# Both expert layers: 32 of 256 tokens by indexed fetch of their chosen rows, 224 dense, the weighted sum made features-by-tokens

## The chip, the cores and the metric

One NeuronCore of one Trainium2 chip runs the whole program. TensorE (PE, with its weight loads shown apart as PEld), VectorE (DVE), ScalarE (ACT), GpSimd (POOL) and SyncE (SP) have an instruction queue each; transfers between HBM and the on-chip memory run on 16 DMA engines. The metric is device microseconds of one execution, as the median of several runs. A second number, the span, is the time from the first to the last instruction of one profiled execution.

## The reference, cut to what matters

The program is two transformer blocks on 256 tokens of 1024 features, all in float32. Each block has an attention mixer and an expert layer; the change touches the two expert layers alone. An expert layer chooses 16 of 16,384 experts for each token and head (8 heads), 128 in all for a token, and sums their value rows:

```python
v1, i1 = lax.top_k(s1, PEER_TOPK)
v2, i2 = lax.top_k(s2, PEER_TOPK)
...
sc, pos = lax.top_k(cand, PEER_TOPK)
eidx = jnp.take_along_axis(cidx, pos, axis=-1)
g = jax.nn.softmax(sc, axis=-1)
u = jnp.take(expert_u, eidx, axis=0)
a = jnp.einsum('thkd,td->thk', u, hc).astype(jnp.float32)
act = (jax.nn.gelu(a, approximate=False) * g).astype(hc.dtype)
vv = jnp.take(expert_v, eidx, axis=0)
return jnp.einsum('thk,thkd->td', act, vv)
```

An expert's number is 128 times its place in the first list plus its place in the second, so the experts form a 128 by 128 grid. `expert_u` and `expert_v` are 64 MB each in each layer.

## The kernel before, in words

The tokens are two tiles of 128. Every expert is computed for every token, and the gate of an expert that a token did not choose is zero. Weights come in units of 128 by 1024 float32 (512 KB), in one long list for the whole program. SP loads them into four `raw` buffers (L290). Each unit is split into two float32r parts: ACT copies `hi` (L302), DVE subtracts to get `lo` (L311), two units ahead of their use. A product is three passes, hi by hi, hi by lo, lo by hi (L330, L331, L332 in `mm3`).

An expert layer (`peer`) goes through these stages:

- Queries: the products of the normed tokens with the query weights, then scores against the keys.
- The u stage: 128 blocks of 128 experts. For each block `project_t` takes a unit of `expert_u`; for each of 8 chunks of features it makes three products, with the unit's chunk as the stationary operand and all 256 tokens as the moving one: 24 products of 256 columns a block. Two blocks share a PSUM bank, and `activated` applies Gelu (L279 by way of `curve`, L1029).
- Meanwhile `top_k` chooses the experts in small steps on DVE, a few of them after each block (lists L1142 to L1146 and what follows). When it is through ("chosen"), `group` makes the gates of four tokens at a time: one-hot rows of the two lists (ACT L997, L998; DVE L1002, L1003), eight float16 products of 128 columns on PE (L1009, L1010), and the product with what is already there of the activations, in `ga` (ACT L1016, DVE L1018). `ga` holds, for each of the 128 blocks, 128 experts by 256 tokens, 128 KB a partition. There are 64 groups, spread over the blocks up to block 122.
- The v stage: 128 blocks again. For each, a unit of `expert_v` is the moving operand in two halves of 512 columns, and the weights in `ga`, split in two parts by `weigh` (ACT L323, DVE L324), are stationary, one tile of 128 tokens at a time (L1073): 12 products of 512 columns a block. The sums come out as tokens by features in four PSUM banks, and are added to x (L509).

Nothing but program order sets who runs when: generators ("tasks") are stepped once after each block by `tick`, and each step records instructions on several engines. An engine works through its own instructions strictly in the recorded order, so an instruction that waits holds up all that stands behind it on its engine. In the last layer the first tile's sums end early, and its last norm and way out run beside the second tile's products.

Of the kernel before, what the change touches and what calls it, by code (L numbers as in the profile page):

```python
# [19 lines left out]
TILES = 2  # L20
# [4 lines left out]
# the second mixer's features, in the order in which they are made  # L25
# [3 lines left out]
# (quarter of the columns, half of k) of an output projection  # L29
# [3 lines left out]
def _columns():  # L33
    """Column ranges of the two packed arrays of constants and small inputs."""
    off, table = 0, {}
    for name, n in (("ident", 128), ("norm_mix", 8), ("norm_ffn", 8), ("norm_ple", 8), ("norm1", 8),
                    ("norm2", 8), ("norm_o", 8), ("b_gate", 2), ("na_q", 1), ("na_k", 1), ("dil_q", 64),
                    ("dil_k", 64), ("cos", 16), ("sin", 16), ("vmask", 8), ("kmask", 32), ("ends", 2)):
# [14 lines left out]
def mixed(lists):  # L53
    """Independent chains of steps, taken in turns."""
    return [step for steps in zip(*lists) for step in steps]

# [16 lines left out]
# The tokens are kept in the order (t % 2, t % 32 // 2, t // 32): a tile holds every second token, so that it holds  # L73
# whole classes of the two wider dilations, and every second one of its rows lies in the same half of the grid's columns.
# [8 lines left out]
def _arrays(a):  # L83
    """Device inputs: the reference's arrays laid out, and constants that depend on shapes alone."""
# [16 lines left out]
    o["meta"] = np.ascontiguousarray(np.asarray(a["meta_tokens_2"], f))  # L101
    o["normf"] = np.ascontiguousarray(np.asarray(a["norm_f_g_2"], f).reshape(1, 1024))
# [9 lines left out]
    # the branches of the first half of the columns first  # L112
# [10 lines left out]
    for i, (un, vn) in enumerate((("peer_expert_u", "peer_expert_v"), ("expert_u_2", "expert_v_2"))):  # L123
        u = np.asarray(a[un], f)[0].reshape(128, 128, 8, 128)
        o[f"u{i + 1}"] = np.ascontiguousarray(u.transpose(0, 3, 2, 1)).reshape(128, 128, 1024)
        o[f"v{i + 1}"] = np.ascontiguousarray(np.asarray(a[vn], f)[0]).reshape(128, 128, 1024)
# [11 lines left out]
    # neighbourhood attention: a half of the grid's columns at a time, and the near quarter of the other half  # L138
# [11 lines left out]
    # dilated attention: all keys, and twice those of the same tile  # L150
# [33 lines left out]
    put(cst, "ends", np.stack([p % 64 >= 48, p % 64 < 16], axis=1))  # L184
    o["cst"] = cst
# [29 lines left out]
class Kernel:  # L215
# [668 lines left out]
    def peer(self, gain, keys, sides_apart, aim, prefetch):  # L884
# [197 lines left out]
        for blk in range(128 - n_last):  # L1082
# [8 lines left out]
            if self.tasks:  # L1091
                self.tick()
# [743 lines left out]
```

## Time and profile before

| what | value |
|---|---|
| timed runs | 2031.79, 2033.11, 2036.97 us; median 2033.11 us |
| profiled execution | span 2031.8 us, 35290 instructions |
| PE busy | 2015.8 us, 13710 matmuls |
| DVE busy | 1448.3 us |
| ACT busy | 1153.0 us |
| POOL busy | 7.6 us |
| DMA | 344.00 MB, mean 169 GB/s |
| u stage, first and second layer | from 277 to 676 us, from 1264 to 1665 us |
| v stage, first and second layer | from 676 to 1035 us, from 1665 to 2024 us |

The profiled execution's span lies at the low end of the three timed runs. "Busy" of PE counts a matmul from its start to its modelled end, and matmuls overlap, so the rate has to be read from how many start in a stretch and not from the share. The starts of the stages are the first and last matmuls of L330 and L1073.

### The profile page before, as it was taken

To read this page: it belongs to the slowest core of one execution; us is meant where nothing else is said; L and a number is where in the kernel's file an instruction comes from. 1 tells how busy PE (TensorE), PEld (TensorE's weight loads), DVE (VectorE), ACT (ScalarE), POOL (GpSimd) and SP (SyncE) were. 2 spreads that over 40 slices of the span, in tenths; PEclk is the share of its full clock that TensorE was granted. 3 is DMA by queue.
4 is the path that set the end of the run, shared out by engine and by line. 5 is a ranking of instruction groups with operands and counts; after the bars stand their busy time and mean duration, and the time that the engine had idled before them with its cause. 6 is when DMAs were issued, how large, how long until landed. Compare 5 with 4: busy or idle time off the path is not lost.

```text
span 2031.8 us, 35290 instructions
## 1 busy us (share of the span) xinstructions
PE 2015.8 (99%) x13710; PEld 1822.6 (90%) x13710; DVE 1448.3 (71%) x3074; ACT 1153.0 (57%) x1867; POOL 7.6 (0%) x14
## 2 busy tenths in 40 slices
PE   8999999999999999999999999999999999999998
PEld 7899999999999888888879989999999998888886
DVE  6866899778889555555576568997889985555555
ACT  5555556577776544444465645465777764444444
POOL 1000000000000000000000000000000000000000
PEclk9999999999999999999999999999999999999999
DMA  7443455544444555565654314555444445555563
GB/s 247 150 152 110 165 177 181 191 156 161 162 166 157 189 185 190 183 196 183 198 191 142 104 52 160 184 177 191 152 160 160 159 170 192 183 191 186 186 202 130
DMA packets 95703, 344.00 MB, mean 169 GB/s; under 512 B 10640, under 2 KB 11936, under 8 KB 95536
## 3 DMA queue, kind: packets, MB, share of 16 engines
q1 hardware_dynamic: 93168, 337.16, 49.5%
q10 hardware_dynamic: 2368, 4.60, 0.7%
q8 instruction: 107, 1.75, 0.3%
q14 instruction: 60, 0.49, 0.1%
HBM read 340.66 MB, written 1.05 MB: 168 GB/s over the span
## 4 chain that ended last, share of the span: by engine, by line
PE 96%; DVE 2%; ACT 1%; issue 0%; DMA 0%; SPq 0%; DVEq 0%; ACTq 0%
PE bank L1073 35%; PE bank L330 18%; PE bank L331 17%; PE bank L332 17%; PE bank L1009 2%; PE bank L1010 1%; PE bank L1661 1%; DVE lo L311 1%; PE bank L489 1%; PE bank L431 0%; PE bank L736 0%; ACT hi L302 0%; PE bank L949 0%; PE bank L682 0%; DMA x<-in_x_dram 0%
## 5 line engine op out<-in xcount | busy, mean ns | idle before, releaser
L302 ACT ACTIVATE hi<-raw 128x1024 fp32r<-128x1024 f32 x639 | 676.4, 1060 | 772.7 <-PE bank L1073 369.9
L311 DVE TENSOR_TENSOR lo<-raw,hi 128x1024 fp32r<-128x1024 f32 x639 | 773.9, 1221 | 231.2 <-ACT hi L302 230.2
L330 PE MATMUL bank<-ht,hi 128*128 128x256 f32 x2336 | 668.9, 286 | 0.0
L331 PE MATMUL bank<-ht,hi 128*128 128x256 f32 x2336 | 655.7, 281 | 0.0
L332 PE MATMUL bank<-ht,lo 128*128 128x256 f32 x2336 | 655.2, 280 | 0.0
L1073 PE MATMUL bank<-hi,ht 128*128 128x512 f32 x2048 | 561.9, 395 | 0.0
L1073 PEld LDWEIGHTS bank<-hi,ht 128*128 128x128 f32 x2048 | 384.3, 188 | 94.8
L330 PEld LDWEIGHTS bank<-ht,hi 128*128 128x128 f32 x2336 | 440.6, 189 | 1.7 <-ACT hi L302 0.3
L331 PEld LDWEIGHTS bank<-ht,hi 128*128 128x128 f32 x2336 | 440.6, 189 | 0.0
L332 PEld LDWEIGHTS bank<-ht,lo 128*128 128x128 f32 x2336 | 439.9, 188 | 0.0
L1073 PE MATMUL bank<-lo,ht 128*128 128x512 f32 x1024 | 323.4, 395 | 0.0
L1073 PEld LDWEIGHTS bank<-lo,ht 128*128 128x128 f32 x1024 | 192.2, 188 | 45.1
L324 DVE TENSOR_TENSOR ht<-ga,ht 128x1024 fp32r<-128x1024 f32 (+2 forms) x78 | 84.1, 1088 | 149.8 <-ACT ht L323 149.7
L1003 DVE TENSOR_SCALAR o<-iota,i1t,pack 128x128 f32<-128x128 f16 x512 | 163.9, 341 | 0.0
L1018 DVE SCALAR_TENSOR_TENSOR ga<-bank,ga 128x216 f32<-128x216 f32 (+30 forms) x128 | 64.9, 507 | 44.4 <-ACT ga L1016 43.6
L997 ACT ACTIVATE away<-iota,i2t 128x128 f16<-128x128 f16 x256 | 87.4, 391 | 0.0
L330 PE MATMUL bank<-hi,ht 128*128 128x512 f32 (+1 forms) x224 | 82.7, 369 | 0.0
L331 PE MATMUL bank<-lo,ht 128*128 128x512 f32 (+1 forms) x224 | 80.7, 360 | 0.8 <-DVE lo L311 0.8
L332 PE MATMUL bank<-hi,ht 128*128 128x512 f32 (+1 forms) x224 | 80.5, 359 | 0.6 <-DVE ht L424 0.6
L1009 PE MATMUL bank<-o,o 128*128 128x128 f16 x512 | 74.3, 223 | 0.0
L323 ACT ACTIVATE ht<-ga 128x1024 fp32r<-128x1024 f32 (+2 forms) x78 | 72.4, 936 | 0.7 <-PE bank L332 0.3
L1010 PE MATMUL bank<-o,o 128*128 128x128 f16 x512 | 72.6, 218 | 0.0
(338 smaller groups left out, 1875.3 us busy)
## 6 DMA issues: line engine op xcount, KB each, us to landing
raw<-in_u_dram SPq DMA_DIRECT2D x256, 512.0 KB, 3.5
raw<-in_v_dram SPq DMA_DIRECT2D x256, 512.0 KB, 4.2
raw<-in_w_qkv_dram SPq DMA_DIRECT2D x30, 512.0 KB, 4.2
raw<-in_w_q_dram SPq DMA_DIRECT2D x24, 512.0 KB, 3.5
raw<-in_w_t_dram SPq DMA_DIRECT2D x21, 512.0 KB, 3.5
raw<-in_w_gates_dram SPq DMA_DIRECT2D x16, 512.0 KB, 3.5
raw<-in_w_branch_dram SPq DMA_DIRECT2D x14, 512.0 KB, 3.5
raw<-in_w_pg_dram SPq DMA_DIRECT2D x8, 512.0 KB, 4.2
```

The costliest lines, as they stand in the source:

```text
L302: self.nc.scalar.activation(parts[0], raw, AF.Copy)
L311: self.nc.vector.tensor_tensor(lo, raw, hi.bitcast(F32), op=OP.subtract)
L323: self.nc.scalar.activation(hi, src, AF.Copy)
L324: self.nc.vector.tensor_tensor(lo, src, hi.bitcast(F32), op=OP.subtract)
L330: mm(out, l[0], r[0], start=start, stop=False, **kw)
L331: mm(out, l[0], r[1], start=False, stop=False, **kw)
L332: mm(out, l[1], r[0], start=False, stop=stop, **kw)
L997: nc.scalar.activation(away[:, j], self.iota, AF.Abs, scale=-1.0, bias=i2t[:, 4 * g + j:4 * g + j + 1])
L1003: nc.vector.tensor_scalar(o1[:, j], self.iota, i1t[:, t:t + 1], pf[:, t:t + 1], op0=OP.is_equal, op1=OP.mult)
L1009: nc.tensor.matmul(b[:, j], o2[:, j], halves[:, :, 1], start=True, stop=False)
L1010: nc.tensor.matmul(b[:, j], o2[:, j], halves[:, :, 0], start=False, stop=True)
L1073: nc.tensor.matmul(acc[tt][n], weights[i][:, ai, j, s], v[vi][:, n], start=blk == 0 and ai == 0 and vi == 0, stop=blk == 127 and ai == 1)
```

## The change

Of the 256 tokens the first 224 (`DENSE`) stay in the dense scheme, the last 32 (`GATHERED`) leave it.

For the 224: the moving operand of the u products is 224 columns, not 256; `ga` is 224 tokens wide; there are 56 groups of gates, not 64. In the v stage the operands change places: a chunk of 128 features of the `expert_v` unit is stationary, and the weights of 224 tokens move. One product of 448 columns takes hi of v with both parts of the weights, and one of 224 columns takes lo of v with hi of the weights; the sums stand as features by tokens in eight PSUM banks, all there are, and are turned back by transposes at the end.

For the 32: `spread_picks` repeats each token's chosen expert numbers and gates four times over the partitions, so that partition 32 g + t holds the picks 32 g to 32 g + 31 of token t. `gathers` then fetches, for each of 32 picks, a [128, 1024] tile of rows of `expert_u` by an indirect DMA from GpSimd (512 KB, a new row-major copy `rows1`, `rows2` in HBM), and DVE reduces its product with the normed tokens to one number a partition. After Gelu and gates, 32 more indirect DMAs fetch rows of `expert_v`, which DVE sums up, weighted. Three buffers hold fetched rows; a reduction comes after every third `tick` in the u stage and after every second one in the v stage. The four shares of each token are added by one product with the constant `fold`. The early end of the first tile in the last layer is gone. (The rest of the diff drops comments and docstrings, so line numbers move.)

```diff
+GATHERED = 32
+DENSE = 256 - GATHERED
+SHARE = 128 // GATHERED
...
-    def project_t(self, ht, out):
+    def project_t(self, ht, out, s=slice(None)):
         w = self.unit(8)
         for k in range(8):
-            self.mm3(out, (w[0][:, k], w[1][:, k]), both(ht, k), k == 0, k == 7)
+            self.mm3(out, (w[0][:, k], w[1][:, k]), both(ht, k, s), k == 0, k == 7)
         self.tick()
...
-        ga = pool.tile([128, 128, 256], F32, name="ga")
+        ga = pool.tile([128, 128, DENSE], F32, name="ga")
...
+        picks = self.ready_picks(pool, n)
...
+        n_groups = DENSE // 4
+        self.start(self.gathers(pool, picks, n))
         for blk in range(128):
...
-            self.project_t(ht, b[:, blk % 2])
+            self.project_t(ht, b[:, blk % 2], dense)
...
-        acc = [[self.bank() for _ in range(2)] for _ in range(TILES)]
+        acc = [self.bank()[:, :2 * DENSE].rearrange("p (s t) -> p s t", s=2) for _ in range(8)]
...
-            for ai, vi in ((0, 0), (0, 1), (1, 0)):
-                for n in halves:
-                    nc.tensor.matmul(acc[tt][n], weights[i][:, ai, j, s], v[vi][:, n],
-                                     start=blk == 0 and ai == 0 and vi == 0, stop=blk == 127 and ai == 1)
+            mm = nc.tensor.matmul
+            mm(acc[c], v[0][:, c], weights[i][:, :, j], start=blk == 0, stop=False, skip_group_check=True)
+            mm(acc[c][:, 1], v[1][:, c], weights[i][:, 0, j], start=False, stop=blk == 127, skip_group_check=True)
...
-        self.drain()
+        self.done.add("second")
+        self.run_until_idle("gathers")
...
+        self.until("summed")
...
+        for c in range(8):
+            for blk, v in last:
+                add_rows(blk, v, c)
+            nc.scalar.activation(corr[:, c], acc[c][:, 1], AF.Copy)
+            nc.vector.tensor_tensor(out[:, c], acc[c][:, 0], corr[:, c], op=OP.add)
+            if c % 4 == 3:
...
+                nc.tensor.matmul(banks[1][128 - GATHERED:, :], self.c("fold"), picks["sum"][:, s], start=True, stop=True)
+                for k in range(4):
+                    for tt in range(TILES):
...
+                        nc.tensor.transpose(banks[tt][:rows, 128 * k:128 * (k + 1)], out[:, 4 * half + k, ts], ident)
+                for tt in range(TILES):
+                    self.add_to_x(tt, 512 * half, banks[tt])
...
         if aim is None:
-            for _ in second:
+            for _ in mixed_steps(self.finish(0), self.finish(1)):
                 pass
...
+    def spread_picks(self, picks, numbers, gates):
...
+        for j, t in enumerate((numbers, gates)):
+            mm(b[:, j], repeat, t, start=True, stop=True)
+        mm(b[:, 2, :TILES], repeat, self.y, start=True, stop=True)
+        yield
+        for g in range(SHARE):
+            rows = slice(GATHERED * g, GATHERED * (g + 1))
+            nc.vector.tensor_copy(picks["index"][rows], b[rows, 0, rows])
+            nc.scalar.activation(picks["gate"][rows], b[rows, 1, rows], AF.Copy)
...
+    EVERY = (3, 2)
+    def gathers(self, pool, picks, n):
...
+        for half in range(2):
+            s = slice(512 * half, 512 * (half + 1))
+            b = self.bank()
+            nc.tensor.matmul(b, self.c("repeat"), self.x[:, 1, s], start=True, stop=True)
+            yield
+            h = picks["normed"][:, s]
+            nc.vector.scalar_tensor_tensor(h, b, picks["y"][:, 1:2], h, op0=OP.mult, op1=OP.mult)
+        tables = (self.d[f"rows{n}"], self.d[f"v{n}"].rearrange("b p d -> (b p) d"))
+        jobs = [(t, j) for t in range(2) for j in range(GATHERED)]
...
+                rows[i] = pool.tile([128, 1024], F32, tag="gathered", name="gathered", bufs=3)
+                nc.gpsimd.indirect_dma_start(out=rows[i], out_offset=None, in_=tables[t],
+                                             in_offset=bass.IndirectOffsetOnAxis(ap=picks["index"][:, j:j + 1], axis=0))
...
+        for i, (t, j) in enumerate(jobs):
+            for _ in range(self.EVERY["second" in self.done]):
+                yield
+            r = rows.pop(i)
+            if t == 0:
+                nc.vector.tensor_tensor_reduce(r, r, picks["normed"], 1.0, 0.0, OP.mult, OP.add, w[:, j:j + 1])
+            else:
+                if j == 0:
...
+                    nc.vector.tensor_scalar(total, r, w[:, :1], None, op0=OP.mult)
+                else:
+                    nc.vector.scalar_tensor_tensor(total, r, w[:, j:j + 1], total, op0=OP.mult, op1=OP.add)
+            fetch(i + 3)
```

How the recorded order moves is seen at three places. First DVE late in the first layer's u stage, before: `lo` is a unit's second part, `o` a one-hot row of a gate group, `ga` the gates or activations.

```order
L311 TENSOR_TENSOR lo<-raw,hi 128x1024
L1018 SCALAR_TENSOR_TENSOR ga<-bank,ga 128x110x4
L1029 TENSOR_TENSOR ga<-ga,bank 128x2x220
L1003 TENSOR_SCALAR o_8183<-iota,i1t,pack 128x128 x2
L1002 TENSOR_SCALAR o_8182<-iota,i2t 128x128
L1003 TENSOR_SCALAR o_8183<-iota,i1t,pack 128x128
L1002 TENSOR_SCALAR o_8182<-iota,i2t 128x128
L1003 TENSOR_SCALAR o_8183<-iota,i1t,pack 128x128
L311 TENSOR_TENSOR lo<-raw,hi 128x1024
```

And now, at about the same block:

```order
L334 TENSOR_TENSOR lo<-raw,hi 128x1024
L1216 ISA gathered,pick_dot<-gathered,repeated 128x1024
L1216 ISA pick_dot 128x1
L1043 SCALAR_TENSOR_TENSOR ga<-bank,ga 128x110x4
L1028 TENSOR_SCALAR o_8065<-iota,i1t,pack 128x128 x2
L1027 TENSOR_SCALAR o_8064<-iota,i2t 128x128
L1028 TENSOR_SCALAR o_8065<-iota,i1t,pack 128x128
L1027 TENSOR_SCALAR o_8064<-iota,i2t 128x128
L1028 TENSOR_SCALAR o_8065<-iota,i1t,pack 128x128
L334 TENSOR_TENSOR lo<-raw,hi 128x1024
```

The reduction of a fetched tile (L1216, in two instructions) stands between two `lo` of every third block, ahead of the gate group's work.

Second, PE in the v stage, a block before, with `ht` the split weights and `hi`, `lo` the unit:

```order
L1073 MATMUL bank<-hi,ht_77 128x512 x2
L1073 MATMUL bank<-lo,ht_77 128x512 x2
L1073 MATMUL bank<-hi,ht_77 128x512 x4
L1073 MATMUL bank<-lo,ht_77 128x512 x2
L1073 MATMUL bank<-hi,ht_77 128x512 x4
```

And now, where one set of four blocks' weights ends (`ht_77`) and the next begins (`ht_78`):

```order
L1100 MATMUL bank<-ht_77,lo 128x224
L1099 MATMUL bank<-ht_77,hi 128x448
L1100 MATMUL bank<-ht_77,lo 128x224
L1099 MATMUL bank<-ht_78,hi 128x448
L1100 MATMUL bank<-ht_78,lo 128x224
```

Long and short products alternate, 16 a block, each with a stationary operand of its own.

Third, near the end of the program on PE, now: `repeated` is the gathered tokens' sum, `cst` the constants, `ga` the turned sums.

```order
L1100 MATMUL bank<-ht_78,lo 128x224
L1136 MATMUL bank<-repeated,cst 32x512
L1141 MATMUL bank<-cst,ga 128x128
L1141 MATMUL bank<-cst,ga 96x128
L1141 MATMUL bank<-cst,ga 128x128
L1141 MATMUL bank<-cst,ga 96x128
```

The fold and eight transposes (four of them shown) come after the last product; before, the program's last PE instruction was a product of L1073.

More of the change, by code (lines that the diff above doesn't have):

```diff
@@ L55, in mixed, with mixed_steps @@
     return [step for steps in zip(*lists) for step in steps]
+def mixed_steps(*gens):
+    gens = list(gens)
+    while gens:
+        gens = [g for g in gens if next(g, gens) is not gens]
+        yield
 def columns(cols):
@@ L244, in until, with run_until_idle @@
         while not all(n in self.done for n in names):
+            self.tick()
+    def run_until_idle(self, name):
+        while any(g.__name__ != name for g in self.tasks):
             self.tick()
@@ L1104, in peer @@
[L1104 to L1116 removed]
+        ident = self.c("ident")
@@ new lines, in peer @@
+        out = flat[:, :8 * DENSE].rearrange("p (c t) -> p c t", c=8)
+        corr = flat[:, 8 * DENSE:16 * DENSE].rearrange("p (c t) -> p c t", c=8)
+        for c in range(8):
+            for blk, v in last:
+                add_rows(blk, v, c)
+            nc.scalar.activation(corr[:, c], acc[c][:, 1], AF.Copy)
+            nc.vector.tensor_tensor(out[:, c], acc[c][:, 0], corr[:, c], op=OP.add)
+            if c % 4 == 3:
+                half = c // 4
+                banks = [self.bank() for _ in range(TILES)]
+                s = slice(512 * half, 512 * (half + 1))
+                nc.tensor.matmul(banks[1][128 - GATHERED:, :], self.c("fold"), picks["sum"][:, s], start=True, stop=True)
+                for k in range(4):
+                    for tt in range(TILES):
+                        ts = slice(128 * tt, min(128 * (tt + 1), DENSE))
+                        rows = ts.stop - ts.start
+                        nc.tensor.transpose(banks[tt][:rows, 128 * k:128 * (k + 1)], out[:, 4 * half + k, ts], ident)
+                for tt in range(TILES):
+                    self.add_to_x(tt, 512 * half, banks[tt])
+                if aim is not None and half == 0:
+                    self.start(self.turn_x(0))
+                    self.tick()
+                    self.all_squares()
@@ L1120, in peer, with ready_picks @@
         pool.release()
-    def top_k(self, score, scratch, i1t, i2t, pack):
+    def ready_picks(self, pool, n):
+        picks = {}
+        picks["normed"] = t = pool.tile([128, 1024], F32, name="repeated")
+        self.nc.scalar.dma_start(t, self.d[f"gain{n}"].to_broadcast([128, 1024]))
+        picks["index"] = pool.tile([128, GATHERED], U32, name="index")
+        for name in ("gate", "dot"):
+            picks[name] = pool.tile([128, GATHERED], F32, name=f"pick_{name}")
+        picks["y"] = pool.tile([128, TILES], F32, name="pick_y")
+        return picks
@@ L1124, in top_k @@
+    def top_k(self, score, scratch, i1t, i2t, pack, picks):
         nc = self.nc
@@ L1215, in turning @@
                 banks.append(b)
+            nc.vector.scalar_tensor_tensor(numbers, chosen[0][:, 128:], 128.0, chosen[1][:, 128:], op0=OP.mult, op1=OP.add)
+            self.start(self.spread_picks(picks, numbers, chosen[2][:, 128:]))
             yield
```

91 lines of the change are left out of this document (53 added, 38 removed).

## The prediction

> **What bounds the kernel now.** I read the page first, its chain of waits, then busy time by stretches, then the timeline of single engines. The page:
>
> ```profile
> span 2031.8 us, 35290 instructions
> PE 2015.8 (99%) x13710; PEld 1822.6 (90%) x13710; DVE 1448.3 (71%) x3074; ACT 1153.0 (57%) x1867; POOL 7.6 (0%) x14
> ...
> PE 96%; DVE 2%; ACT 1%; issue 0%; DMA 0%; SPq 0%; DVEq 0%; ACTq 0%
> PE bank L1073 35%; PE bank L330 18%; PE bank L331 17%; PE bank L332 17%; PE bank L1009 2%; PE bank L1010 1%; PE bank L1661 1%; DVE lo L311 1%; PE bank L489 1%; PE bank L431 0%; PE bank L736 0%; ACT hi L302 0%; PE bank L949 0%; PE bank L682 0%; DMA x<-in_x_dram 0%
> ```
>
> The chain that ends last is PE for 96% of the span, and 87% of it are the products that the change makes shorter. The stretches say at what rate they run (columns: stretch, its length, then busy us and instructions of PE, PEld, DVE, ACT, POOL, granted clock, DMA share, GB/s):
>
> ```profile
> 285.00:390.00 105.00, 105.00 (x897) 105.00 (x896) 97.78 (x308) 59.73 (x65) 0.00 (x0) 1.00 0.56 190
> ...
> 530.00:660.00 130.00, 130.00 (x1210) 128.53 (x1210) 115.29 (x282) 91.52 (x206) 0.00 (x0) 1.00 0.48 162
> ...
> 676.00:1034.00 358.00, 358.00 (x1541) 288.14 (x1540) 192.11 (x166) 167.84 (x166) 1.05 (x3) 1.00 0.59 189
> ```
>
> A 256-column product starts every 105/897 = 0.117 us in the u stage, a 512-column one every 358/1541 = 0.232 us in the v stage: both 0.454 to 0.457 ns a column. So PE is paid by the column there, and DVE is the one to watch: 93% busy in the first row, 89% in the second, 54% in the v stage. Where gates are made, PE's timeline shows a block and its group:
>
> ```profile
> 402.75 0.23 PE L1009 MATMUL bank<-o,o 128*128 128x128 f16 x1
> ...
> 657.86 0.23 PE L1009 MATMUL bank<-o,o 128*128 128x128 f16 x1
> ...
> 658.30 0.36 PE L330 MATMUL bank<-ht,hi 128*128 128x256 f32 x1
> 658.50 0.28 PE L331 MATMUL bank<-ht,hi 128*128 128x256 f32 x1
> ...
> 661.24 0.23 PE L1009 MATMUL bank<-o,o 128*128 128x128 f16 x1
> ...
> 1420.72 0.23 PE L1009 MATMUL bank<-o,o 128*128 128x128 f16 x1
> ```
>
> Block and group take 661.24 - 657.86 = 3.38 us, the group 0.53 of it (from 657.86 to 658.50, less one product of 0.12), so the block alone 2.85; before the first group it is 24 x 0.117 = 2.81. The first groups come at 402.75 and 1420.72, about 44 and 54 blocks after the stages begin.
>
> **The change part by part: what PE saves.** By the column, 224 columns would take 0.102 us. But each product needs its own stationary operand, and the trace shows what loading one costs when the product is short:
>
> ```profile
> 1104.36 0.22 PE L1566 MATMUL bank<-spl,r_ones 128*128 128x128 f32 x1
> 1104.42 0.39 PE L1567 MATMUL bank<-spl,r_tri 128*128 128x384 f32 x1
> 1104.65 0.28 PE L1572 MATMUL bank<-sph,r_sel 128*128 128x256 f32 x1
> ...
> 1184.86 0.39 PE L1597 MATMUL bank<-sv,at 128*128 128x64 f32 x2
> ...
> 1185.53 0.28 PE L1597 MATMUL bank<-sv,at 128*128 128x64 f32 x1
> ```
>
> L1566 and L1567, 128 and 384 columns, take 0.29 us from start to start of what follows; the 384 columns are 0.174 of it, which leaves 0.116 for 128 columns that would stream in 0.058. Six products of 64 columns (L1597 to L1599, each with a load) take 1185.53 - 1184.86 = 0.67, 0.112 each. So I take 0.112 as the least time between two products with a full load each. In the u stage it binds: 24 x 0.112 = 2.69 us a block. That saves 0.12 us on 44 blocks and 0.16 on 212: 39 us, not the 90 that the columns promise. In the v stage a block becomes eight pairs of 448 and 224 columns: the first streams 0.203 and hides the load, the second is held to 0.112: 8 x 0.315 = 2.52 us, from 12 x 0.232 = 2.79. Over 256 blocks 69 us. Sixteen groups of gates fewer: 16 x 0.53 = 8.5 us. Sum 116.5.
>
> (The Trainium skill, "TensorE: Matmul & The Clock Gate", section "LDWEIGHTS (loading the stationary operand)", gives columns / 1.2 in ns, 107 for 128. By it a u block would be 2.57 us and a v block 2.48, an estimate of about 40 us more saved if nothing else held it; the row says 112 to 116, and I go by the row.)
>
> **What is added on PE.** Float32 products run in two instructions; their prices:
>
> ```profile
> 236.75 0.59 PE L386 MATMUL bank<-diag,all_ones 128*128 128x256 f32 x2
> 237.18 1.05 PE L949 MATMUL bank<-ga 128*128 128x128 f32 x8
> 237.99 0.36 PE L330 MATMUL bank<-ht,hi 128*128 128x256 f32 x1
> ```
>
> 256 columns take 0.43 us, so 512 take 0.86; an instruction of 128 takes 0.10 to 0.11. For each layer: two repeats of x and two folds, 4 x 0.86; numbers, gates and scales repeated, 0.66; sixteen transposes, 1.8: 5.9, together 11.8 us.
>
> **The ends.** The last layer's way out, now:
>
> ```profile
> 2023.67 0.40 PE L1073 MATMUL bank<-hi,ht 128*128 128x512 f32 x1
> ...
> 2024.20 0.68 DVE L509 TENSOR_TENSOR x<-x,bank 128x512 f32<-128x512 f32 x1
> ...
> 2026.58 0.16 DVE L339 TENSOR_TENSOR newton<-y 128x1 f32<-128x1 f32 x1 [0.50 <-ACT y L346]
> ...
> 2027.35 0.75 DVE L1738 SCALAR_TENSOR_TENSOR x<-x,y,norm_f 128x512 f32<-128x512 f32 x1
> ```
>
> From the last product to the end are 7.8 us, for one tile; the other had gone ahead. Now both come last: beside the fold and transposes (counted above) one more addition of 0.6 to 0.7, a second chain from 2026.58 to 2027.35 (0.8), a second final scaling (0.75), and ACT's copy ahead of the transposes, partly under the fold: 2.6 us. At the first layer's end one addition, 0.7. At each passage from u to v the sums take all eight banks, so PE waits for the last pair's Gelu and product: 0.5 each. Together 4.3 us.
>
> **What is added on DVE**, which is what may eat the gain. From start to start:
>
> ```profile
> 622.61 1.22 DVE L311 TENSOR_TENSOR lo<-raw,hi 128x1024 fp32r<-128x1024 f32 x1
> 623.74 0.61 DVE L1018 SCALAR_TENSOR_TENSOR ga<-bank,ga 128x440 f32<-128x440 f32 x1
> 624.27 0.60 DVE L1003 TENSOR_SCALAR o<-iota,i1t,pack 128x128 f32<-128x128 f16 x2
> ...
> 625.62 1.22 DVE L311 TENSOR_TENSOR lo<-raw,hi 128x1024 fp32r<-128x1024 f32 x1
> ...
> 627.28 0.60 DVE L1029 TENSOR_TENSOR ga<-ga,bank 128x440 f32<-128x440 f32 x1
> 627.80 0.60 DVE L1003 TENSOR_SCALAR o<-iota,i1t,pack 128x128 f32<-128x128 f16 x2
> ```
>
> A `lo` costs 1.13, the gates' product 0.53, one-hot rows of a group 1.35, the activations' product 0.52. The reduction of a fetched tile is not in the trace. Its nearest rows:
>
> ```profile
> L311 DVE TENSOR_TENSOR lo<-raw,hi 128x1024 fp32r<-128x1024 f32 x639 | 773.9, 1221 | 231.2 <-ACT hi L302 230.2
> L597 DVE TENSOR_REDUCE hv<-sq 128x16 f32<-128x1024 f32 x5 | 6.1, 1213 | 0.0
> ```
>
> One pass is 1.2 us, product and sum apart would be 2.43; I take 1.25 (one pass and a read of the result), and 2.43 as the far end. Below 1.13 no row of that width goes. Late in the u stage three blocks hold three `lo`, two groups, two gates' products, one of the activations and one reduction: 3.39 + 2.70 + 1.06 + 0.52 + 1.25 = 8.92 us, where PE needs 3 x 2.69 + 2 x 0.53 = 9.13. DVE would be 98% full, and it works in order and waits for ACT:
>
> ```profile
> DVE ga L1018 <- ACT ga L1016: 27.7, 28, 1.9
> DVE ga L1029 <- ACT bank L279: 11.4, 26, 0.9
> ```
>
> That is 39 us idle between 400 and 660 us, 15%, most of it because DVE is ahead. If a third stays, a block takes 0.15 us longer: over the last 100 or so of the 158 blocks with groups 15 us. In the blocks before the groups DVE needs 97.78/105 x 2.81 = 2.62 of 2.69 us: 0.03 x 98 = 3. So 18 us, between 0 and (at 2.43, for some 51 reductions in the two u stages, 51 x 1.2 more) 80. In the v stage two blocks need 2 x 1.13, half of a `weigh` (0.6) and 1.25, 4.1 of 5.04 us: hidden, and with 0.9 us to spare.
>
> **DMA.** A fetch is 512 KB like a unit. In the v stage a unit every 2.52 us and a fetch every 5.04 are 208 + 104 = 312 GB/s; the trace has carried more:
>
> ```profile
> 3.00:13.00 10.00, 7.39 (x25) 5.86 (x26) 6.62 (x10) 4.65 (x7) 4.06 (x4) 1.00 0.94 365
> ...
> raw<-in_v_dram SPq DMA_DIRECT2D x256, 512.0 KB, 4.2
> ...
> gla<-in_cst_dram ACTq DMA_DIRECT2D x1, 512.0 KB, 8.3
> ```
>
> Three buffers give a fetch three intervals less a reduction: 3 x 5.04 - 1.25 = 13.9 us in the v stage, twice that in the u stage. The trace holds no indirect DMA; transfers of that size land in 3.5 to 8.3 us. I take it as hidden, at nothing; a reduction that waits for its rows would hold up every `lo` behind it on DVE, and so PE.
>
> **Sum.** 116.5 - 11.8 - 4.3 - 18 = 82. The profiled span of 2031.8 less 82 is 1950; the median of the runs is 1.3 above that span, which is within their spread. I forecast **1950 us**.
>
> **Rivals.** (1) *The load does not bind at 224 columns*: PE by the column alone. A v block is 8 x 0.305 = 2.44, 21 us less; in the u stage DVE's 2.62 to 2.97 us a block leaves perhaps 4 more. 1925. For it: loads overlap the products in this trace (PEld 90%). Against it: the two rows above.
>
> (2) *DVE becomes the bound of the u stage*, since a reduction takes two passes or the fetches cost DVE time: 51 x 1.2 = 62 us more, 2012. For it: DVE at 98% has no slack. Against it: the list of instructions shows one wide instruction and one of a single column.
>
> (3) *Fetches come late*: slower. Place: the v stage, where some 76 reductions in both layers come every second block. With a latency G the interval is (G + 1.25)/3 instead of 5.04 us. The 82 us are gone when that is 6.12, so at G = 17; at 20 us it costs 76 x 2.04 = 155, 2105. For it: no run shows what an indirect fetch of 128 rows costs GpSimd. Against it: twice the slowest landing of that size. (The Trainium skill, "SBUF — State Buffer", section "SBUF: two separate sides", says GpSimd cannot write the descriptors of its DMAs while DVE runs an operation in a two-port mode; the one-hot rows L1003 would be such. No run here shows it; it would raise G.)
>
> (4) *The parts cancel* and nothing is measured: a smaller form of (2) and (3).
>
> **How the numbers follow.** The forecast 0.65, (1) 0.09, (2) 0.12, (3) 0.11, (4) 0.03. Range: 1920, just under rival (1), to 2012, rival (2); it leaves out (3). Runs of this kernel tell 0.3%, 6 us, from no change. Faster is the forecast, (1) and (2): 0.86; slower (3): 0.11; the rest 0.03.
>
> **What would show it.** Starts of u products 0.112 us apart before the groups, and blocks with a group near 3.25; v pairs 0.315 apart. A spacing of 0.102 speaks for (1). L1216 longer than 1.5 us, or idle PE ahead of L353 products until DVE's `lo`, for (2). DVE idle ahead of L1216 or L1228 until a DMA, or landings over 14 us, for (3). After the last product about 12 us to the end. I am wrong if the u stage, now 399 and 401 us, isn't some 12 to 25 us shorter in each layer, or the v stage, now 359, isn't about 325.

## The result, and the profile after

| | before | with the change |
|---|---|---|
| median of the runs | 2034.25 us (4 runs) | 1939.79 us (4 runs, 1939.57 to 1945.5) |
| ratio | | 0.9542, 95% interval 0.9527 to 0.9557 |
| profiled span | 2031.8 us | 1938.2 us |
| u stage, first product to first of the v stage, by layer | 398.9, 401.0 us | 376.2, 379.9 us |
| v stage, first to last product, by layer | 359.0, 358.2 us | 334.2, 327.4 us |
| between the v stage of one layer and the u stage of the next | 229.4 us | 230.2 us |
| start of the last product to the end | 8.1 us | 12.4 us |

The kernel is faster by 4.6%: 93.6 us of span, where 82 were forecast. The stages are read from the starts of the products: L330 became L353, L331 and L332 became L354 and L355, and L1073 became L1099 (448 columns) and L1100 (224). The other lines that moved: `lo` L311 to L334, the groups' one-hot rows L1003 to L1028, the products of the gates L1018 to L1043 and of the activations L1029 to L1054. New are the fetch L1205, the reduction L1216 and the weighted sum L1228.

The page of the changed kernel, its busy times and its chain of waits:

```profile
span 1938.2 us, 37562 instructions
PE 1913.2 (99%) x14666; PEld 1815.0 (94%) x14666; DVE 1551.3 (80%) x3188; ACT 1131.0 (58%) x1833; POOL 181.8 (9%) x142
...
PE 87%; DVE 9%; ACT 2%; issue 1%; DMA 1%; DVEq 0%; ACTq 0%
```

PE still sets the time, though DVE's part of the chain has grown from 2 to 9%. Three stretches of the changed kernel (columns as in the prediction's stretches), in the u stage before the groups, late in it, and the first layer's v stage:

```profile
285.00:390.00 105.00, 105.00 (x942) 104.94 (x940) 98.94 (x315) 61.59 (x71) 0.00 (x0) 1.00 0.64 197
530.00:650.00 120.00, 120.00 (x1165) 119.39 (x1164) 117.37 (x264) 81.91 (x178) 12.50 (x14) 1.00 0.76 233
654.00:988.00 334.00, 331.69 (x2065) 308.08 (x2065) 231.20 (x214) 169.30 (x175) 55.66 (x34) 1.00 0.74 258
```

A product starts every 105/942 = 0.1115 us, not every 0.102 as 224 columns alone would have it. (That the weight loads, PEld, fill the stretch, 104.94 of 105, does not show that they bind: with 256 columns they filled it too, 105.00 of 105. Experiments 7 and 8 decide.) Late in the u stage DVE is busy 97.8% of the time (117.37 of 120 us), and PE all of it. PE's timeline shows the pieces, a block's last products and a group, and then pairs of the v stage:

```profile
411.79 0.27 PE L353 MATMUL bank<-ht,hi 128*128 128x224 f32 x1
411.90 0.28 PE L354 MATMUL bank<-ht,hi 128*128 128x224 f32 x1
412.01 0.27 PE L355 MATMUL bank<-ht,lo 128*128 128x224 f32 x1
412.12 0.23 PE L1034 MATMUL bank<-o,o 128*128 128x128 f16 x1
412.19 0.22 PE L1035 MATMUL bank<-o,o 128*128 128x128 f16 x1
412.25 0.22 PE L1034 MATMUL bank<-o,o 128*128 128x128 f16 x1
...
703.86 0.38 PE L1099 MATMUL bank<-ht,hi 128*128 128x448 f32 x1
704.08 0.26 PE L1100 MATMUL bank<-ht,lo 128*128 128x224 f32 x1
704.18 0.38 PE L1099 MATMUL bank<-ht,hi 128*128 128x448 f32 x1
```

Products 0.11 apart in the u stage; a pair of 448 and 224 columns takes 0.32, eight of them 2.53 us a block. Twenty-four products by 0.1115 are 2.68 us, and most blocks with a group take 3.12 or 3.20. The group's own float16 products, each with a 128 by 128 operand of its own too, start 0.06 apart, and their loads are recorded as 96 ns long, those of L353 as 191: 0.1115 is not a least time of every product.

The fetches and the reductions, each with its durations in ns (least, median, greatest) and where it ran:

```profile
L1216 DVE CUSTOM_DVE_ANT_0 gathered<-gathered,repeated x64: 1204/1217/1224, 413.5 to 1638.7; 128x1024 f32<-128x1024 f32 x64
L1216 DVE DVE_READ_ACCUMULATOR2_ANT pick_dot<- x64: 70/82/89, 414.6 to 1639.8; 128x1 f32 x64
```

```profile
L1205 POOL DMA_INDIRECT gathered<-in_v_dram,index x64: 937/1677/1783, 665.9 to 1790.2; - x64
...
DMA to landing us min/median/max: 4.1/5.9/9.0
```

The reduction is one pass and a read, 1.22 + 0.08 us, and a fetch lands in at most 9.0 us (median 5.1 for the u table, 7.9 for the v table), under the allowance of 13.9. What is left of a loss stands in the first layer's v stage. First the weight loads that waited there (us in total, times, longest), then DVE's and PE's timelines at 763 us:

```profile
PEld bank L1100 <- DVE lo L334: 6.3, 17, 0.6
```

```profile
762.31 1.09 DVE L347 TENSOR_TENSOR ht<-ga,ht 128x896 fp32r<-128x896 f32 x1 [2.10 <-ACT ht L346]
763.32 1.28 DVE L1228 SCALAR_TENSOR_TENSOR repeated<-gathered,pick_dot,repeated 128x1024 f32<-128x1024 f32 x1
764.52 2.35 DVE L334 TENSOR_TENSOR lo<-raw,hi 128x1024 fp32r<-128x1024 f32 x2
```

```profile
765.35 0.38 PE L1099 MATMUL bank<-ht,hi 128*128 128x448 f32 x1
765.79 0.37 PE L1100 MATMUL bank<-ht,lo 128*128 128x224 f32 x1
```

Every fourth block, DVE waits 2.1 us for ACT's half of the split of the next weights (`weigh`, L347), then does the split and a weighted sum, and only then a `lo` that PE already needs: the product of 224 columns starts 0.44 us after the one before it instead of 0.22. Sixteen blocks of the first layer take 2.86 us in place of 2.53. In the second layer the sums fall between other blocks, and four blocks of 2.81 to 2.86 are all there are.

### The profile page after: what moved, and what is told of

It reads as the page before. It is cut to its first block, busy times and chain, and to the rows that moved or that the text cites. A ratio compares the mean times of both kernels' runs of the same rounds, so it can differ in the third digit from the quotient of the medians.

```text
span 1938.2 us, 37562 instructions
## 1 busy us (share of the span) xinstructions
PE 1913.2 (99%) x14666; PEld 1815.0 (94%) x14666; DVE 1551.3 (80%) x3188; ACT 1131.0 (58%) x1833; POOL 181.8 (9%) x142
## 3 DMA queue, kind: packets, MB, share of 16 engines
HBM read 408.90 MB, written 1.05 MB: 212 GB/s over the span
## 4 chain that ended last, share of the span: by engine, by line
PE 87%; DVE 9%; ACT 2%; issue 1%; DMA 1%; DVEq 0%; ACTq 0%
PE bank L1099 21%; PE bank L353 16%; PE bank L354 16%; PE bank L355 16%; PE bank L1100 10%; DVE lo L334 4%; DVE o L1028 1%; PE bank L1034 1%; PE bank L1035 1%; PE bank L1775 1%; DVE gathered L1216 1%; DVE ga L1043 1%; PE bank L512 1%; DVE repeated L1228 1%; ACT hi L325 0%
## 5 line engine op out<-in xcount | busy, mean ns | idle before, releaser
L334 DVE TENSOR_TENSOR lo<-raw,hi 128x1024 fp32r<-128x1024 f32 x639 | 772.2, 1218 | 104.2 <-ACT hi L325 103.8
L353 PE MATMUL bank<-ht,hi 128*128 128x224 f32 (+1 forms) x2336 | 654.8, 280 | 0.0
L1099 PE MATMUL bank<-ht,hi 128*128 128x448 f32 x2048 | 650.1, 376 | 0.5 <-DVE ht L347 0.5
L355 PE MATMUL bank<-ht,lo 128*128 128x224 f32 (+1 forms) x2336 | 643.2, 275 | 1.2 <-DVE lo L334 1.2
L354 PE MATMUL bank<-ht,hi 128*128 128x224 f32 (+1 forms) x2336 | 642.8, 275 | 0.0
L1100 PE MATMUL bank<-ht,lo 128*128 128x224 f32 x2048 | 544.6, 266 | 1.6 <-DVE lo L334 0.3
L355 PEld LDWEIGHTS bank<-ht,lo 128*128 128x128 f32 x2336 | 447.5, 192 | 1.9 <-DVE lo L334 1.7
L353 PEld LDWEIGHTS bank<-ht,hi 128*128 128x128 f32 x2336 | 447.0, 191 | 1.7 <-ACT hi L325 0.3
L354 PEld LDWEIGHTS bank<-ht,hi 128*128 128x128 f32 x2336 | 447.4, 192 | 0.0
L1099 PEld LDWEIGHTS bank<-ht,hi 128*128 128x128 f32 x2048 | 384.1, 188 | 35.8 <-DVE ht L347 0.9
L1100 PEld LDWEIGHTS bank<-ht,lo 128*128 128x128 f32 x2048 | 391.1, 191 | 7.5 <-DVE lo L334 7.5
L1205 POOL DMA_INDIRECT gathered<-in_rows_dram,index x64 | 69.2, 1082 | 1224.2 <-DVE o L1028 440.6
L347 DVE TENSOR_TENSOR ht<-ga,ht 128x896 fp32r<-128x896 f32 (+2 forms) x78 | 75.6, 979 | 125.5 <-ACT ht L346 125.5
L1028 DVE TENSOR_SCALAR o<-iota,i1t,pack 128x128 f32<-128x128 f16 x448 | 142.6, 340 | 0.0
L1205 POOL DMA_INDIRECT gathered<-in_v_dram,index x64 | 105.0, 1640 | 227.5 <-DVE repeated L1228 191.3
L354 PE MATMUL bank<-lo,ht 128*128 128x512 f32 (+1 forms) x224 | 80.1, 358 | 2.7 <-DVE lo L334 2.7
L353 PE MATMUL bank<-hi,ht 128*128 128x512 f32 (+1 forms) x224 | 81.7, 365 | 0.5 <-ACT hi L325 0.5
L355 PE MATMUL bank<-hi,ht 128*128 128x512 f32 (+1 forms) x224 | 80.0, 357 | 0.6 <-DVE ht L447 0.6
L1228 DVE SCALAR_TENSOR_TENSOR repeated<-gathered,pick_dot,repeated 128x1024 f32<-128x1024 f32 x62 | 79.3, 1279 | 0.0
L1216 DVE CUSTOM_DVE_ANT_0 gathered<-gathered,repeated 128x1024 f32<-128x1024 f32 x64 | 77.7, 1215 | 0.0
```

The costliest lines, as they stand in the source:

```text
L334: self.nc.vector.tensor_tensor(lo, raw, hi.bitcast(F32), op=OP.subtract)
L353: mm(out, l[0], r[0], start=start, stop=False, **kw)
L354: mm(out, l[0], r[1], start=False, stop=False, **kw)
L355: mm(out, l[1], r[0], start=False, stop=stop, **kw)
L1028: nc.vector.tensor_scalar(o1[:, j], self.iota, i1t[:, t:t + 1], pf[:, t:t + 1], op0=OP.is_equal, op1=OP.mult)
L1099: mm(acc[c], v[0][:, c], weights[i][:, :, j], start=blk == 0, stop=False, skip_group_check=True)
```

## The experiments

The first three take the change apart: only the operands of the weighted sum swapped, only 224 columns, and everything but the fetched tokens. Stage times are quoted beside the totals, because the totals differ by up to 5 us in a stretch between the two expert layers whose code is the same (3, below). A kernel's stages are read from one profiled execution; where nothing in a stage changed they repeat closely (the first u stage is 376.1 or 376.2 us in the change and in runs 2, 4, 6, 8 and 9).

**1. Swap alone.** Every token dense, nothing fetched:

```
-DENSE = 256 - GATHERED
+DENSE = 256
-            self.start(self.spread_picks(picks, numbers, chosen[2][:, 128:]))
-        self.start(self.gathers(pool, picks, n))
-        self.until("summed")
-                nc.tensor.matmul(banks[1][128 - GATHERED:, :], self.c("fold"), picks["sum"][:, s], start=True, stop=True)
```

> All 256 tokens stay dense, nothing is fetched; only the weighted sum is made features-by-tokens (products of 512 and 256 columns). Theory (the swap pays only where the operand is narrower than 256 tokens): u stages as before, 399 and 401 us; a v block 8 x (0.232 + 0.117) = 2.79 us, as before; the later way out and the 16 transposes of a layer cost about 8 us, so 2040 us, slower than before by 0.4%. Rival (half as many pairs of products and the wider moving operand pay by themselves, since a load is hidden better): v block under 2.70, time under 2015.

Measured 2033.59 us, ratio 0.9999 (0.9990 to 1.0009). The first layer's v stage:

```profile
673.60:1031.70 358.10, 357.33 (x2064) 313.88 (x2063) 193.82 (x171) 170.38 (x172) 0.00 (x0) 1.00 0.60 190
```

358.3 us from first to last product, against 359.0, and 2.77 us a block, against 2.80: a third more products (16 a block, not 12) and nearly the same time, as the columns are the same. The theory holds, and the rival, which needed a block under 2.70, falls. The total came out 6 us below the 2040 expected: the last product is followed by 11.5 us, 3.4 more than before, but the u stages were 396.1 and 398.3, each about 2.7 shorter than before although their products are the same. Blocks with a group took 3.34 instead of 3.38 us. Why is not settled.

**2. 224 columns alone.** Fetched tokens as in the change, the sum in the old order:

```
+            s = slice(128 * tt, min(128 * (tt + 1), DENSE))
...
+                    nc.tensor.matmul(acc[tt][n][:rows], weights[i][:, ai, j, s], v[vi][:, n],
+                                     start=blk == 0 and ai == 0 and vi == 0, stop=blk == 127 and ai == 1)
...
+            nc.tensor.matmul(acc[1][n][128 - GATHERED:, :], self.c("fold"), picks["sum"][:, 512 * n:512 * (n + 1)],
+                             start=True, stop=True)
```

> 32 tokens fetched and 224 dense as in the change, but the weighted sum in the old order: tokens stationary (128 and 96 columns), 512 columns moving, the fetched sums folded into the last bank. Theory: the u stages keep their gain (376 and 380 us); the v stage keeps its 12 x 0.232 = 2.79 us a block, since no column of the moving operand has gone, so 2031.8 - 44 + 3.4 for the folds = 1991 us. Rival (the fewer columns of the second load shorten the v stage too): v block 2.5 to 2.65, 1940 to 1970.

Measured 1988.64 us, ratio 0.9784 (0.9769 to 0.9799), near the theory's 1991. Its first v stage:

```profile
653.40:1011.80 358.40, 358.40 (x1546) 268.21 (x1546) 230.47 (x210) 168.28 (x171) 55.10 (x37) 1.00 0.69 240
```

The u stages are 376.1 and 379.2 us, as in the change, the v stage is 358.5, as before: with tokens as the stationary operand, 32 of them fewer save nothing, while loads (PEld) are busy 268 us only. So the swap is worth nothing with 256 tokens and 49 us with 224 (1988.64 to 1939.79), and the narrower operand 45 us without the swap: the two together make the 94.

**3. Nothing fetched.** The change without spreading the numbers, the repeat of x, fetches, reductions and sums:

```
-            self.start(self.spread_picks(picks, numbers, chosen[2][:, 128:]))
-        self.start(self.gathers(pool, picks, n))
-        self.until("summed")
```

> As the change, but the 32 tokens' expert output is left out: no numbers spread, no repeat of x, no fetch, no reduction, no weighted sum of fetched rows (the folds stay and add a copy of x instead). It prices all the added work at once. Theory (PE sets the time, DVE's and POOL's work is hidden but for some 9 us in which lo comes late): 1938 - 4.8 for spread and repeat - 9 = 1924 us. Prediction's charge of 18 us on DVE: 1915. If DVE had become the bound (rival 2): 1875 or less. If nothing of it is on the path: 1933.

Measured 1929.28 us, ratio 0.9485 (0.9470 to 0.9499). By stages the change is longer than this kernel by 2.4 and 5.2 us in the u stages (373.9, 374.7 here) and 5.0 and 1.2 in the v stages (329.2, 326.2 here): 13.8 us. Of these, 4.8 are PE's own products for repeat and numbers (2.4 a layer by the prediction's prices), which leaves 9.0 for DVE's lateness: 0 and 2.8 in the u stages, 5.0 and 1.2 in the v stages. That fits what PE's loads waited for in the change: a `lo` for 6.3 us in the first v stage, 1.7 and 1.3 in the second layer's two stages, and there 0.7 for the first split weights. By stages the expected 4.8 + 9 is what was found. The total fell by 10.5 only, midway between the theory's 1924 and the 1933 of "nothing of it is on the path", because the stretch between the layers, whose code is the same, took longer here than in the change:

```profile
988.00:1218.50 230.50, 227.01 (x1577) 202.19 (x1575) 159.40 (x294) 133.21 (x247) 1.04 (x3) 1.00 0.41 127
```

```profile
980.20:1215.90 235.70, 231.50 (x1577) 205.87 (x1575) 159.39 (x294) 133.09 (x247) 1.04 (x3) 0.98 0.40 122
```

The first row is of the change, the second of this kernel: the same 1577 products, a granted clock of 1.00 and 0.98, 5 us. The fetched tokens' work on DVE, 143 us of busy time (1551.3 against 1408.3), cost 9 us in all.

**4. The sums one block later in the first layer.**

```
                     while "second" not in self.done:
                         yield
+                    if n == 1:
+                        yield
```

> As the change, with one more step of waiting ahead of the first weighted row of the first layer, so that the sums of fetched rows fall between the blocks in which the weights are split, as they do in the second layer. Theory (lo is late in every fourth block since the split of the weights and a sum stand ahead of it on DVE): 16 blocks of 2.86 become 2.53, 5 us, 1934 us. Rival (those blocks are long for another reason, the transfers or the clock): 1939, blocks of 2.86 stay.

Measured 1934.60 us, ratio 0.9520 (0.9507 to 0.9533). DVE at the same place:

```profile
759.88 1.09 DVE L347 TENSOR_TENSOR ht<-ga,ht 128x896 fp32r<-128x896 f32 x1 [2.10 <-ACT ht L346]
760.89 1.22 DVE L334 TENSOR_TENSOR lo<-raw,hi 128x1024 fp32r<-128x1024 f32 x1
762.02 1.28 DVE L1230 SCALAR_TENSOR_TENSOR repeated<-gathered,pick_dot,repeated 128x1024 f32<-128x1024 f32 x1
```

The wait for ACT is there as before, but a `lo` now comes ahead of the sum (L1230 here). The first layer's v stage is 328.4 us instead of 334.2, its loads wait for no `lo`, and the other stages are as they were to within 0.1 us. So those 16 blocks were long by the order on DVE, which has the same work in both kernels.

**5. The reduction in two passes.**

```
-                nc.vector.tensor_tensor_reduce(r, r, picks["normed"], 1.0, 0.0, OP.mult, OP.add, w[:, j:j + 1])
+                nc.vector.tensor_tensor(r, r, picks["normed"], op=OP.mult)
+                nc.vector.tensor_reduce(w[:, j:j + 1], r, AX.X, OP.add)
```

> As the change, but each reduction of a fetched tile is made in two passes of DVE, a product and then a sum: 1.13 + 1.21 us instead of 1.22 + 0.08. About 26 of a layer's 32 reductions fall into the u stage. DVE was busy 111.7 of 120 us (410 to 530) and 117.4 of 120 us (530 to 650) there in the first layer, 87.4 of 90 and 114.8 of 117 in the second, so of 0.35 us more a block it has 0.03 to 0.22 left. Theory (DVE is just not the bound): 15 us in the first layer, 18 in the second, v stages as before, 1972 us. Prediction's rival 2 by its own sum: 51 x 1.2, 2000. If DVE's fullness doesn't matter at all: 1940.

Measured 1992.70 us, ratio 0.9789 (0.9773 to 0.9806): 53 us more than the change, nearer to rival 2's sum than to the theory's. Late in the two u stages, and what the loads waited for in the first:

```profile
530.00:670.00 140.00, 131.25 (x1212) 126.86 (x1211) 139.52 (x277) 85.69 (x186) 13.13 (x14) 1.00 0.68 212
...
1480.00:1640.00 160.00, 148.21 (x1360) 142.78 (x1359) 159.26 (x334) 100.10 (x223) 14.07 (x15) 0.99 0.65 199
```

```profile
PEld bank L355 <- DVE lo L334: 13.3, 23, 0.8
```

DVE is busy 139.5 of 140 us and PE only 131: the bound has passed from one to the other. The u stages are 395.5 and 404.4 us, 19 and 25 more than in the change; for the 27 and 24 reductions in them that is 0.7 and 1.0 us each of the 1.05 added. The theory's mistake was to count DVE's idle time as usable slack. The rest is 7 us in the v stages (in the second layer four blocks of 4.05 to 4.16 us, where a reduction falls behind the split) and 3 us between the layers.

**6. One buffer for fetched tiles.**

```
-                rows[i] = pool.tile([128, 1024], F32, tag="gathered", name="gathered", bufs=3)
+                rows[i] = pool.tile([128, 1024], F32, tag="gathered", name="gathered", bufs=1)
```

(and one fetch ahead instead of three)

> As the change, but one buffer for fetched tiles instead of three: the next fetch starts when the sum before it has read the buffer. Theory (fetches are hidden since three of them are under way, rival 3's mechanism): a sum needs 1.28 us and a fetch about 5 to 6 us to land, so the interval becomes 6.3 to 7.3 us; in the u stage it fits in three blocks, in the v stage, where two blocks are 5.06, some 36 sums of a layer cost 1.2 to 2.2 us each: 86 to 160 us more, 2025 to 2100, slower than or as before. Rival (the fetch's length does not reach PE, because parts of the weights are made ahead): 1940 to 1950.

Measured 2120.55 us, ratio 1.0414 (1.0397 to 1.0432): slower than before. DVE in the v stage:

```profile
700.04 1.29 DVE L1227 SCALAR_TENSOR_TENSOR repeated<-gathered,pick_dot,repeated 128x1024 f32<-128x1024 f32 x1 [1.13 <-DMA gathered<-in_v_dram,index]
701.24 2.35 DVE L334 TENSOR_TENSOR lo<-raw,hi 128x1024 fp32r<-128x1024 f32 x2
707.45 1.29 DVE L1227 SCALAR_TENSOR_TENSOR repeated<-gathered,pick_dot,repeated 128x1024 f32<-128x1024 f32 x1 [3.85 <-DMA gathered<-in_v_dram,index]
708.65 2.35 DVE L334 TENSOR_TENSOR lo<-raw,hi 128x1024 fp32r<-128x1024 f32 x2
```

A sum every 7.4 us, of which 1.3 are the sum: from the sum's end to the next one's start 6.1 us pass. The u stages stay at 376 and 381 us; the v stages grow to 420.1 and 422.1, 86 and 95 more. The 181 us lie above the 86 to 160 expected: the sums come later than the 6.3 to 7.3 us assumed, and the granted clock in these v stages was 0.94 and 0.95, where it was 1.00 in the change; how much of the excess is the clock's is open. This is rival 3's mechanism at work. By its formula three buffers and the 7.9 us in which v rows land in the change allow a sum every (7.9 + 1.3)/3 = 3.1 us, where 5.06 on the mean are needed.

**7. Twice as many tokens.**

```
-GATHERED = 32
+GATHERED = 64
-    EVERY = (3, 2)
+    EVERY = (1, 2)
```

> 64 tokens fetched and 192 dense, a reduction at every step of the u stage, a sum at every second of the v stage. By PE alone: u blocks before the groups still 24 x 0.112 = 2.68 us if the load binds (24 x 0.087 = 2.09 if columns did), v block 8 x (0.174 + 0.112) = 2.29, eight groups fewer: 8 + 77 us less, 1853 us. Theory (DVE, 98% full in the u stage already, becomes the bound there): late u blocks of about 3.8 us, u stage some 45 to 50 us longer, v stage 37 shorter: about 1960 us, slower than with 32 tokens. Rival (DVE can take it): below 1900.

Measured 1957.09 us, ratio 0.9623 (0.9607 to 0.9639), slower than with 32. Three stretches, early and late in the first u stage and in the first v stage:

```profile
290.00:390.00 100.00, 100.00 (x898) 100.00 (x897) 93.88 (x293) 57.06 (x67) 0.00 (x0) 1.00 0.64 197
520.00:640.00 120.00, 108.00 (x974) 103.14 (x974) 118.04 (x261) 68.74 (x148) 33.74 (x32) 1.00 0.86 293
690.00:850.00 160.00, 158.17 (x1089) 156.12 (x1089) 135.91 (x120) 84.03 (x85) 52.24 (x34) 1.00 0.94 334
```

192 columns start every 100/898 = 0.1114 us, just as 224 do: the load binds, not the columns. Late in the u stage PE is busy 108 of 120 us and DVE 118. u stages of 403 and 408 us (27 and 28 longer), v stages of 312 and 305 (22 shorter each, where 128 blocks of 2.29 us instead of 2.53 would make it 31). Theory and 1960 us come out. This tried one spread of the fetches only; the transfers, at 0.94 of their time in the last row, might have become the next limit, which no run tests.

**8. The 448 columns in two products.** One product per part of the weights. The kernel leaves part of the sum out, presumably because both products start in the same bank; all instructions are issued.

```
-            mm(acc[c], v[0][:, c], weights[i][:, :, j], start=blk == 0, stop=False, skip_group_check=True)
+            for h in range(2):
+                mm(acc[c][:, h], v[0][:, c], weights[i][:, h, j], start=blk == 0, stop=False, skip_group_check=True)
```

> As the change, but in the v stage the product of 448 columns is made as two of 224 with the same stationary operand: the same columns, a third more loads and instructions. Theory (a full load keeps products 0.112 us apart, whatever they stream below 247 columns): v block 24 x 0.112 = 2.68 instead of 2.53 us, 256 x 0.16 = 40 us more, 1979 us. Rival (PE is paid by the column): 2.44 to 2.53, 1940 us. If a repeated load of the same operand is free or skipped: also 1940.

Measured 1973.72 us, ratio 0.9692 (0.9676 to 0.9708). PE in the v stage:

```profile
704.04 0.39 PE L1100 MATMUL bank<-ht,hi 128*128 128x224 f32 x2
704.26 0.27 PE L1101 MATMUL bank<-ht,lo 128*128 128x224 f32 x1
704.38 0.39 PE L1100 MATMUL bank<-ht,hi 128*128 128x224 f32 x2
```

Three products in 0.34 us where the pair took 0.316, 2.68 us a block instead of 2.53. The same columns cost 34 us more for half as many loads again. By stages it is 13 and 18 us (347.2 and 345.6), and 4 more between the layers at a granted clock of 0.98; the first layer's 13 are less than the 20 expected because no load waits for `lo` in its longer blocks. So the theory's 1979 is near, and loading the same operand again is neither skipped nor free.

**9. The fetched tiles spread otherwise**, the version that the runs point to:

```
-    EVERY = (3, 2)
+    EVERY = (5, 2)
...
+            while "second" in self.done and self.at % 2:
+                yield
```

(`self.at` is the number of the v stage's block.)

> As the change, with the fetched tiles spread otherwise: a reduction at every fifth step of the u stage instead of every third (what is left follows in the v stage), and in the v stage only behind even blocks, never behind the split of the weights. Theory (what is left of the added work's price is lo that comes late, 5 us in the first layer's v stage and some 2 and 4 us late in the u stages): 1939 - 11 = 1928 us. If only the order in the v stage counts: 1934, as with the shift alone.

Measured 1933.34 us, ratio 0.9509 (0.9491 to 0.9526): the fastest of the complete kernels, 0.35% under the change, though not clear of runs 4 and 10 (its own runs are 1931.18 to 1937.94). Its v stages:

```profile
654.00:982.00 328.00, 327.16 (x2063) 307.82 (x2064) 242.23 (x236) 169.06 (x174) 73.78 (x45) 1.00 0.82 280
1593.00:1919.00 326.00, 326.00 (x2057) 307.24 (x2058) 242.77 (x238) 166.36 (x169) 77.43 (x47) 1.00 0.81 277
```

Stages of 328.5 and 326.3 us with more work on DVE than in the change (242 against 231 us), and in all four stages one wait of 0.2 us for a `lo`. The second u stage is 2.8 us shorter, the first one is not, though 2 us were expected of it. Together that is nearly 10 us by the stages, of the 11 expected; the total shows 6.5, the stretch between the layers being 3 us longer at a granted clock of 0.99, so that the total alone would fit the 1934 of the order in the v stage just as well.

**10. And x repeated by transfers.**

```
-            nc.tensor.matmul(b, self.c("repeat"), self.x[:, 1, s], start=True, stop=True)
+        for g in range(SHARE):
+            nc.gpsimd.dma_start(copy[GATHERED * g:GATHERED * (g + 1)], self.x[128 - GATHERED:, 1])
```

> As the one before, and the 32 rows of x are repeated to 128 partitions by four transfers instead of two float32 products a layer. Theory (PE sets the time, so its 4 x 0.86 us come off in full): 3.4 us less than the one before, 1924 us. Rival (DVE, which waits for the rows, holds up lo): no less, or more.

Measured 1934.64 us, ratio 0.9512 (0.9498 to 0.9526): no different, where 1924 was expected. The u stages are 1.1 us shorter each (375.1, 375.9) of the 1.7 expected, and the v stages 1.3 and 1.4 longer: in each one block takes 3.98 us, where ACT loads two function tables (1.28 us each) just ahead of the split of the weights. Most of PE's time came off, and a new coincidence took it back.

## Why the prediction was right, and where its steps were not

The sign, the mechanism and the time (1950 for 1939.79, 0.5%) were right, but two terms were wrong in opposite directions, by 20 and 10 us, so part of the closeness is luck. By stages, from the prediction's terms:

| | forecast | measured |
|---|---|---|
| u stages (39 and 8.5 saved; 4.8 for numbers and repeat, 18 for DVE, 1 for passages added) | -23.7 | -43.8 |
| v stages (69 saved; half of folds and transposes, 3.5, added) | -65.5 | -55.6 |
| all else (the other half, 3.5, and 3.3 at the ends) | +6.8 | +5.8 |
| sum | -82.4 | -93.6 |

- *"87% of it are the products that the change makes shorter"*: too wide. L330 to L332 are a helper's lines that other stages use too; the four stages that change are 1517 of 2032 us, 75%. No term of the sum hangs on it.
- *"I take 0.112 as the least time between two products with a full load each"*: right, 0.1115, and by two more runs: 192 columns keep the same spacing (7), two products of the same operand cost two spacings (8). With nothing fetched the u stages save 25.0 and 26.3 us, 51 against the 47.5 of the sum. Rival 1 falls. The Trainium skill, "TensorE: Matmul & The Clock Gate", section "LDWEIGHTS (loading the stationary operand)", gives columns / 1.2 in ns, 107 for 128 columns; the spacing measured here, 111.5 ns at a granted clock of 1.00, is 4% above it.
- *Pairs at 0.315 and 2.52 us a block*: right, 0.316 and 2.53. The form matters: 224 columns without the swap give the v stage nothing (2), the swap without them nothing either (1).
- *"If a third stays, a block takes 0.15 us longer", 15 of the 18 us charged to DVE*: wrong. The fill was right, 97.8% measured for 98% forecast, and a third of the waits did stay. Of 39 us in which DVE waited for ACT between 400 and 660 us, this is what was left after (400 to 654), 13.4 us:

```profile
DVE ga L1043 <- ACT ga L1041: 6.5, 9, 2.1
DVE ga L1054 <- ACT bank L302: 5.9, 12, 0.8
DVE lo L334 <- ACT hi L325: 1.0, 2, 0.5
```

  But a wait adds to a block only where DVE has no room for it, and these lay where it had room. Some 10 of the 13.4 us fall before 530 us, where DVE was busy 93% (it had waited 25 there before); where it was 98% full, behind 530, it had waited 13 before and waited some 3 now:

```profile
410.00:530.00 120.00, 120.00 (x1168) 119.37 (x1167) 111.71 (x275) 88.10 (x190) 13.29 (x13) 1.00 0.72 229
```

  Our reading, not tested by itself, is that DVE had waited because it was ahead; the less it is ahead, the more often it finds its operands ready. Adding the mean share of waits to the fill was the mistake. Lateness cost 0 and 2.8 us in the u stages instead of 18 (3). The edge is near all the same: 1.05 us more a reduction cost 44 us there (5).
- *"In the v stage ... hidden, and with 0.9 us to spare"*: wrong by 6 us (5.0 and 1.2 by run 3), on the other side. The sum over two blocks is right, but it left out the order: the split of the weights waits 2.1 us for ACT once in four blocks, and whatever is queued behind it makes `lo` late. Moving the sums by one block (4) or keeping them off those blocks (9) takes it away. The other 3.7 us of the shortfall have nothing to do with the fetches, for they are missing without them as well: run 3 saves 29.8 and 32.0 us in the v stages, 61.8 and not 65.5. Some 1.7 of them are the pause of the products between the two halves of the features, for fold, transposes and in the first layer a turn of x: about 4.0 and 1.9 us, where before it was 0.8 in the first layer alone, so 5.2 more and not 3.5. About 1 us is rounding in the forecast's 69, and 0.8 a single late block of run 3's first layer.
- *Rival 2*: its price was about right, 53 us measured for 62 (5), but its condition did not come true: the reduction is one pass of 1.22 us.
- *Rival 3*: refuted for this kernel, with G at 7.9 us in the median for the v table, 9.0 at most, and not 17, and shown to be a mechanism that decides once buffers are few (6). The rule of the Trainium skill cited there ("SBUF — State Buffer", "SBUF: two separate sides") would delay fetches beside the one-hot rows; what GpSimd needed to issue a fetch was shorter in the u stage, where these rows run (median 0.94 us), than for most fetches of the v table (1.68), so no run here shows a loss by these rows.
- *About 12 us after the last product*: 12.4. Of the price at the passage from u to v (0.5 each, for the eight banks) the first layer paid 0.1 and the second 0.7: the last u block took 2.82 and 3.38 us instead of 2.68, and the load that waited there waited for DVE's split of the first weights (`ht`, L347).

## What to carry to other kernels

A narrower moving operand pays by the column only until the next weight load ends, here 0.112 us, or by an estimate from 0.454 ns a column some 247 columns; below that, join two products on one stationary operand before taking off more columns. Columns count only where they stand on the moving side, so an operand's place in the product decides whether dropping rows of it saves anything. Whether a nearly full second engine costs time is not told by the sum of its work alone: at 98% it cost 0 and 2.8 us a stage, and at 69% it cost 5.0 us where a wait and other work stood in its queue ahead of the instruction that the first engine needed.

## What the runs showed of the hardware that was not expected

- A second load of the operand that is already in place takes as long as a new one: 0.112 us a product with the same operand twice in a row (8).
- A fetch of 128 rows of 4 KB by index lands in 4.1 to 9.0 us, median 5.9 (5.1 from the u table, 7.9 from the v table), while the transfers move 213 GB/s on the whole and up to 313, and occupies GpSimd for 0.93 to 2.0 us; for the v table it mostly took 1.68 us, for the u table 0.94. Why they differ is open.
- The same 1577 products between the two layers took 230 to 236 us in different kernels, with a granted clock of 1.00 to 0.98. That is up to 0.3% of the whole, as much as some of the edits here, so differences of 3 to 5 us were read from the stages. Executions of one kernel differ so too: the change took 1945.5 us at a mean granted clock of 0.995 and 1939.57 to 1939.94 at 0.998 to 0.999.
- Products of 256 columns in the late u stage ran at 2.85 us a block before and at 2.81 with only the v stage's operands swapped (1), while ahead of the groups the blocks were equal (2.82 in the first layer, 2.85 in the second); the cause is open.
